# Two-layer hybrid backbone with expert-choice MoE: read-back of the residual streams tied to the last gather, final norm on one engine, output sums in one piece

## The chip, the cores and the metric

The kernel runs on one core of a Trainium2 chip. The metric is the device time of one execution, in microseconds (us). TensorE (PE), VectorE (DVE), ScalarE (ACT), GpSimd (POOL) and SyncE (SP) run their own queues in order and wait for each other through semaphores. Plain transfers here are issued by SP (queue q1 of the profile), the gathers, scatters and the read-back by POOL (queue q0); both use the same 16 DMA engines.

## The reference, cut to what matters

Two layers over 512 latent tokens and 256 context tokens of width 1024. A layer adds an attention and convolution branch to the streams, and then a mixture of experts: each of 16 experts takes the tokens for which its router score is highest (64 latent ones; in the first layer 32 context ones too), runs a SwiGLU on them, and its weighted rows are added to the tokens that they came from. The output is a last RMS norm.

```python
def ec_ffn(h, router_w, w_gate, w_up, w_down):
    aff = jax.nn.softmax((h @ router_w).astype(jnp.float32), axis=-1)
    top_aff, idx = lax.top_k(jnp.swapaxes(aff, 1, 2), cap)
    xg = jax.vmap(lambda hb, ib: hb[ib])(h, idx)                    # gather
    hid = jax.nn.silu(einsum(xg, w_gate)) * einsum(xg, w_up)
    y = einsum(hid, w_down) * top_aff[..., None]
    return zeros.at[idx].add(y)                                      # sum into the tokens
...
for li in range(2):
    xl = xl + g1 * (mix(xl, xc) @ w_o)
    xl = xl + g2 * ec_ffn(rmsnorm(xl, norm2_g) * (1 + sc2) + sh2, ...)   # xc alike, in layer 0 only
return rmsnorm(xl, final_norm_g)
```

## The kernel before, in words

All weights are float32 and are read once, in 1 MB pieces through a ring of slots; one expert has four pieces of gate and up (`load_gu`) and two of down (`load_d`). The order of TensorE's instructions is the order of the program; the other queues, SP's and POOL's among them, are ordered by a planner that runs through the program with estimated times and takes of the instructions that it thinks ready the one that stands first.

The expert part of a layer is one loop (e = 0 to 16, at the end of `layer`). Iteration e has on TensorE: `gate_up(e, 0)` (gate and up products of expert e for the latent rows); `hid_t(e-1)` (transposes of the hidden values of the expert before); a first `fill`; `columns(e+1)` (transposes of the gathered rows of the next expert into `xgT`); in layer 0 `gate_up(e, 1)` (context rows); a second `fill`; `down(e-1)` in `finish`. The rows of an expert are gathered by `gather` from a table in DRAM into `xg`, a single buffer: the gather for e+2 may start when `columns(e+1)` has read the one before. In layer 1 a gather and a `columns` serve two experts, so they stand in every second iteration only, `columns` in the odd ones.

There are two ways in which an expert's rows reach the streams. In layer 0 the experts 0 to 11 add theirs into copies of the streams in DRAM (`accs`), by a scatter that accumulates (lines 1072 and 1073). After that the six stream tiles `xl` (four) and `xc` (two), 512 KB each, are read back from `accs` by POOL's queue (line 1194). Experts 12 to 15 of layer 0, and all of layer 1, are summed on TensorE instead: `combine` makes pieces, each of two matmuls (tile `cb`, two buffers) with a one-hot matrix, and an addition into half a tile of the stream by VectorE (line 1118). Pieces wait in the list `todo`, and `fill(n)` issues n of them: eight pieces for a pair of experts, after each second expert.

In layer 0 the read-back stands in iteration 13, behind `gather(15)` in the program; the additions that need it begin in iteration 15. The planner put four of the six transfers ahead of that gather in POOL's queue.

After the last expert of layer 1, `final` does for each of four tiles: two pieces, the sum of squares on ScalarE, the factor `rs` (line 147, a power on POOL), the multiplication by `rs` and by the gain `fg` (it lies in the tile `xg`), and the store. Tiles 1 and 3 do the multiplication in one instruction of VectorE, tiles 0 and 2 in one of ScalarE and one of POOL.

Of the kernel before, what the change touches and what calls it, by code (L numbers as in the profile page):

```python
# [13 lines left out]
AF = mybir.ActivationFunctionType  # L14
OP = mybir.AluOpType
# [11 lines left out]
NE = 16  # L27
# [17 lines left out]
def hybrid_kernel(ctx: ExitStack, tc: tile.TileContext, a, out):  # L45
    nc = tc.nc
    V, S, G, PE, Q = nc.vector, nc.scalar, nc.gpsimd, nc.tensor, nc.sync
# [57 lines left out]
    def bcast(src, off, parts, n):  # L105

        return bass.AP(tensor=src.tensor, offset=src.offset + off, ap=[[0, parts], [1, n]])
# [34 lines left out]
    def rstd_of(ssq, n, inv):  # L142

        t = small.tile([128, 16], F32, name="rs_t")
        r = small.tile([128, 16], F32, name="rs_r")
        V.tensor_scalar(t[:, :n], ssq, inv, EPS, op0=OP.mult, op1=OP.add)
        G.tensor_tensor(r[:, :n], t[:, :n], mhalf[:, :n], op=OP.pow)  # L147
        return r
# [91 lines left out]
    def layer(li, ada):  # L240
        upd = li == 0
# [517 lines left out]
        @early(-30)  # L759
        def load_gu(e, q=Q):  # L760
            wgu = wgus[e] = []
            for w in ("exp_w_gate", "exp_w_up"):
                ws = []
                for k in range(0, KD, 4):
                    t = slot([128, 4, FF])
                    q.dma_start(t, a[w][li, e, k // 4])
                    ws += [t[:, i] for i in range(4)]
                wgu.append(ws)

        def load_d(e, q=Q):  # L770
            wd = wds[e] = []
            for k in range(0, 4, 2):
                t = slot([128, 2, D])
                q.dma_start(t, a["exp_w_down"][li, e, k // 2])
                wd += [t[:, 0], t[:, 1]]
# [5 lines left out]
        for r in range(len(streams)):  # L781
            t = rt.tile([128, D], F32, name=f"g1_{r}")
# [6 lines left out]
        for r, grp in enumerate(streams):  # L789
            t = rt.tile([48, len(grp) * 64], F32, name=f"affT{r}")  # L790
# [208 lines left out]
        xgs, xgTs = {}, {}  # L999

        def gather(e):
            if not upd and e % 2:
                return
            xg = xgs[e] = ex.tile([ng, D], F32, name="xg", bufs=1)
            c = e if upd else e // 2
            G.indirect_dma_start(out=xg, out_offset=None, in_=tabx[li],
                                 in_offset=bass.IndirectOffsetOnAxis(ap=gidx[:ng, c:c + 1], axis=0))

        def columns(e):

            if not upd and e % 2:
                xgTs[e] = xgTs[e - 1]
                return
            xg = xgs[e]
            xgT = xgTs[e] = ex.tile([128, KD, ng], F32, name="xgT")
            for k0 in range(0, KD, 4):
                ps = ps_tp()
                for k in range(4):
                    PE.transpose(ps[:, k * ng:(k + 1) * ng], xg[:, (k0 + k) * 128:(k0 + k + 1) * 128], ident[:ng, :ng])  # L1019
                for k in range(4):  # L1020
                    s, b = m.a2[:, k0 + k], m.b2[:, k0 + k]
                    n = CAPL if upd else ng
                    S.activation(xgT[:, k0 + k, :n], ps[:, k * ng:k * ng + n], AF.Identity, bias=b[:, 0:1], scale=s[:, 0:1])  # L1023
                    if upd:
                        V.tensor_scalar(xgT[:, k0 + k, n:], ps[:, k * ng + n:(k + 1) * ng], s[:, 1:2], b[:, 1:2],
                                        op0=OP.mult, op1=OP.add)
# [3 lines left out]
        def gate_up(e, r):  # L1030

            xgT, wgu = xgTs[e], wgus[e]
            ps = ps_mm()
            if r == 0:
                n = FF
                c0 = 0 if upd else (e % 2) * CAPL
                for k in range(KD):
                    for s in range(2):
                        mm(ps[64 * s:64 * s + 64, :], xgT[:, k, c0:c0 + CAPL], wgu[s][k], k == 0, k == KD - 1)
            else:  # L1040
                n = FF // 2
                for k in range(KD):
                    for q in range(4):
                        mm(ps[32 * q:32 * q + 32, :n], xgT[:, k, CAPL:],
                           wgu[q // 2][k][:, (q % 2) * n:(q % 2 + 1) * n], k == 0, k == KD - 1)
            gh = hids[e, r] = ex.tile([128, FF], F32, name="gh")
            S.activation(gh[64:128, :n], ps[0:64, :n], AF.Silu)  # L1047
            V.tensor_tensor(gh[0:64, :n], ps[64:128, :n], gh[64:128, :n], op=OP.mult)  # L1048

        def hid_t(e, r):  # L1050
            n = FF if r == 0 else FF // 2
            hid = hids[e, r]
            ps = ps_tp()
            for c in range(n // 128):
                PE.transpose(ps[:, c * 64:c * 64 + 64], hid[0:64, c * 128:(c + 1) * 128], ident[:64, :64])  # L1055
            hT = hTs[e, r] = ex.tile([128, n // 2], F32, name=f"hTe{r}")
            S.copy(hT, ps[:, :n // 2])  # L1057
# [66 lines left out]
        rs = range(len(streams))  # L1124
# [16 lines left out]
        def final(steps, p):  # L1141

            fg = p.tile([ng, D], F32, name="xg", bufs=1)
            Q.dma_start(fg, bcast(a["final_norm_g"], 0, 128, D))
            sq2 = p.tile([128, 4, 2], F32, name="sq2f", bufs=1)
            def block(tb):
                x = X["xl"][tb]
                for hf in range(2):
                    steps[2 * tb + hf]()
                    j = p.tile([128, 512], F32, name="gh")  # L1150
                    S.activation(j, x[:, hf * 512:(hf + 1) * 512], AF.Square, accum_out=sq2[:, tb, hf:hf + 1])
                sq = small.tile([128, 1], F32, name="ssq")
                V.tensor_tensor(sq, sq2[:, tb, 0:1], sq2[:, tb, 1:2], op=OP.add)
                rs = rstd_of(sq, 1, 1.0 / D)
                if tb % 2:
                    V.scalar_tensor_tensor(x, x, rs[:, 0:1], fg, op0=OP.mult, op1=OP.mult)  # L1156
                else:
                    S.activation(x, x, AF.Identity, scale=rs[:, 0:1])
                    G.tensor_tensor(x, x, fg, op=OP.mult)
                Q.dma_start(out[tb * 128:(tb + 1) * 128, :], x)  # L1160

            for tb in range(4):
                block(tb)

        def fill(n):
            for f in todo[:n]:
                f()
            del todo[:n]
# [5 lines left out]
        for e in range(NE + 1):  # L1174
            if e + 1 < NE and e + 1 not in wgus:
                load_gu(e + 1, G if upd and e == 1 else Q)
            if e < NE:
                if e not in wds:
                    load_d(e, Q if upd or e > 1 else G)
                gate_up(e, 0)  # L1180
            if e:
                for r in rs:
                    hid_t(e - 1, r)
                fill(3 if upd else 2)
            if e < NE:
                if e + 1 < NE:
                    columns(e + 1)
                if e + 2 < NE:
                    gather(e + 2)
                if upd and e == NE - 3:  # L1190

                    for x, acc in ((X["xl"], accs[0]), (X["xc"], accs[1])):
                        for i, t in enumerate(x):
                            G.dma_start(t, acc[i * 128:(i + 1) * 128, :])
                if upd:
                    gate_up(e, 1)
            if e:
                fill(3 if upd else 2)
                finish(e - 1)
        if upd:  # L1200
            fill(len(todo))
# [10 lines left out]
    with tc.manual_schedule(engines={mybir.EngineType.PE}):  # L1212
        for li in range(DEPTH):
            layer(li, ada)
# [93 lines left out]
```

## Time and profile before

Three runs took 1455.22, 1456.85 and 1459.57 us; the median is 1456.85 us. The profiled execution took 1453.06 us, of which its span from the first to the last instruction is 1451.3 us.

| engine or queue | busy us | share of the span |
|---|---|---|
| TensorE matmul | 1280.1 | 88% |
| TensorE weight load | 800.0 | 55% |
| VectorE | 687.3 | 47% |
| ScalarE | 517.6 | 36% |
| GpSimd | 242.2 | 17% |
| queue q1 (SP), of 16 DMA engines | | 50.7% |
| queue q0 (POOL), of 16 DMA engines | | 7.3% |

321.14 MB are moved, 221 GB/s over the span. The expert loop of layer 0 runs from about 523 to 848 us, that of layer 1 from about 1203 us to the end. A busy share is an average over stages with different limits; within a stage one looks for the wait that ended last.

### The profile page before, as it was taken

Reading aid. Unit: us, or ns where it says so; the run is one execution under the profiler, and the core shown is the slowest. Engines: PE = TensorE matmul, PEld = TensorE weight load, DVE = VectorE, ACT = ScalarE, POOL = GpSimd, SP = SyncE. Lnnn points to the kernel's source line nnn. Section 1 sums busy time; section 2 is a strip of 40 time slices with the busy share of each in tenths; the row PEclk is TensorE's granted clock in tenths of the full one; section 3 lists DMA queues with packets and bytes.
Section 4 is the critical chain, followed back from the end, with each engine's and each line's share of the span. In section 5 each row is a group of like instructions: output and inputs, shape, how many; then the busy total and the mean of one; then the engine's idle time right before and its main releaser. Section 6 shows DMA issues by size and latency. Waiting matters only on the chain. (4 is left out here: it accounts for less than half of the span.)

```text
span 1451.3 us, 21505 instructions
## 1 busy us (share of the span) xinstructions
PE 1280.1 (88%) x8542; PEld 800.0 (55%) x8542; DVE 687.3 (47%) x1516; ACT 517.6 (36%) x1095; POOL 242.2 (17%) x266
## 2 busy tenths in 40 slices
PE   3989989999999869999996969998999958999994
PEld 0768866666678624444443438876777843343331
DVE  1545356566743632222222474847776351333435
ACT  2523145455533322222222143436666322232222
POOL 1111001212210222222221020102232011111203
PEclk9989999999999979999998969999999978999998
DMA  8523315444732489999999310110012857999991
GB/s 355 187 99 116 149 63 215 175 182 182 291 145 82 190 314 361 367 373 370 373 371 399 133 56 32 71 62 1 1 41 70 341 222 308 419 418 420 419 416 62
DMA packets 56195, 321.14 MB, mean 221 GB/s; under 512 B 8720, under 2 KB 10384, under 8 KB 22560
## 3 DMA queue, kind: packets, MB, share of 16 engines
q1 hardware_dynamic: 45664, 286.75, 50.7%
q0 software_dynamic: 10432, 33.04, 7.3%
q8 instruction: 67, 1.10, 0.3%
q14 instruction: 32, 0.26, 0.1%
HBM read 304.52 MB, written 15.24 MB: 220 GB/s over the span
## 5 line engine op out<-in xcount | busy, mean ns | idle before, releaser
L59 PE MATMUL mm<-slot,xgT 128*64 128x512 f32 (+1 forms) x2048 | 290.6, 493 | 0.8 <-DMA slot<-in_exp_w_up_dram 0.7
L59 PE MATMUL mm<-hT,w 128*128 128x512 f32 (+1 forms) x1176 | 230.8, 356 | 3.0 <-POOL w L140 2.0
L59 PEld LDWEIGHTS mm<-hT,w 128*128 128x128 f32 x1176 | 192.6, 192 | 37.5 <-POOL w L140 2.4
L59 PEld LDWEIGHTS mm<-slot,xgT 128*64 128x64 f32 (+1 forms) x2048 | 104.8, 125 | 170.5 <-issue 143.8
L59 PE MATMUL mm<-slot,hTe 128*32 128x256 f32 (+1 forms) x1024 | 146.8, 490 | 0.8 <-ACT hTe L1057 0.8
L1048 DVE TENSOR_TENSOR gh<-mm,gh 64x512 f32<-64x512 f32 (+1 forms) x48 | 29.0, 604 | 218.4 <-ACT gh L1047 218.4
L1047 ACT ACTIVATE gh<-mm 64x512 f32<-64x512 f32 (+1 forms) x48 | 24.9, 518 | 278.1 <-PE tp L1055 171.8
L59 PE MATMUL mm<-wo,mixb 128*128 128x512 f32 x360 | 98.2, 409 | 2.3 <-DVE mixb L140 1.4
L59 PEld LDWEIGHTS mm<-slot,hTe 128*32 128x32 f32 (+1 forms) x1024 | 48.9, 123 | 88.7 <-issue 71.3
L694 ACT COPY pt<-tp 128x512 f32<-128x512 f32 (+1 forms) x120 | 64.9, 542 | 81.3 <-PE tp L691 80.2
L691 PE MATMUL tp<-ident,p 128*128 128x128 f32 x552 | 87.1, 283 | 5.5 <-ACT pt L694 2.3
L1023 ACT ACTIVATE xgT<-tp,modT,a 128x64 f32<-128x64 f32 (+1 forms) x192 | 70.1, 425 | 58.7 <-PE tp L1019 54.3
L681 POOL TENSOR_SCALAR p<-p,sm 128x768 f32<-128x768 f32 (+1 forms) x30 | 58.5, 1951 | 124.3 <-DVE sm L680 116.0
L691 PEld LDWEIGHTS tp<-ident,p 128*128 128x128 f32 x552 | 61.1, 142 | 27.1 <-issue 18.0
L59 PEld LDWEIGHTS mm<-wo,mixb 128*128 128x128 f32 x360 | 65.1, 191 | 16.2 <-DVE mixb L140 2.2
L59 PE MATMUL ada<-slot,sT 128*32 128x512 f32 x384 | 53.7, 678 | 22.9 <-DMA slot<-in_ada_w_dram 22.9
L59 PE MATMUL sc<-kt,qh 96*128 96x512 f32 (+1 forms) x324 | 69.7, 348 | 0.0
L139 ACT CAST w<-slot 128x1024 fp32r<-128x1024 f32 x30 | 31.4, 1046 | 100.1 <-PE mm L59 73.8
L59 PE MATMUL sc<-kst,qst 128*128 128x256 f32 (+1 forms) x288 | 48.2, 298 | 20.5 <-DVE mx L678 12.7
L670 DVE TENSOR_REDUCE mx<-sc 128x1 f32<-128x768 f32 (+1 forms) x60 | 51.0, 851 | 26.9 <-PE sc L59 25.9
L59 PE MATMUL cb<-yp,pl 128*128 128x512 f32 x160 | 53.1, 449 | 11.5 <-DVE xl L1118 9.2
L1101 POOL TENSOR_SCALAR pl<-tok,st 128x512 fp32r<-128x512 f32 (+1 forms) x21 | 32.9, 1575 | 171.9 <-PE cb L59 171.8
(246 smaller groups left out, 1772.9 us busy)
## 6 DMA issues: line engine op xcount, KB each, us to landing
slot<-in_exp_w_gate_dram SPq DMA_DIRECT2D x62, 1024.0 KB
slot<-in_exp_w_up_dram SPq DMA_DIRECT2D x62, 1024.0 KB
slot<-in_exp_w_down_dram SPq DMA_DIRECT2D x62, 1024.0 KB
slot<-in_ada_w_dram SPq DMA_DIRECT2D x48, 1024.0 KB
slot<-in_win_dram SPq DMA_DIRECT2D x14, 1024.0 KB
slot<-in_wo_dram SPq DMA_DIRECT2D x8, 1024.0 KB
tabx<-xn POOLq DMA_DIRECT2D x10, 512.0 KB
xt<-in_x_dram SPq DMA_DIRECT2D x4, 512.0 KB
```

The source lines that it names most:

```text
L59: PE.matmul(o, l, r, start=start, stop=stop, skip_group_check=True)
L139: (hi or V.tensor_copy)(out[0], x)
L670: V.tensor_reduce(mx, sc[:, :n], axis=AX.X, op=OP.max, negate=True)
L681: (G if s and self.kind == "mla" else V).tensor_scalar(p[:, :n], p[:, :n], sm, None, op0=OP.mult)
L691: PE.transpose(ps[:, b * 128:(b + 1) * 128], p[:, (b0 + b) * 128:(b0 + b + 1) * 128], ident)
L694: S.copy(o, ps[:, :n * 128])
L1023: S.activation(xgT[:, k0 + k, :n], ps[:, k * ng:k * ng + n], AF.Identity, bias=b[:, 0:1], scale=s[:, 0:1])
L1047: S.activation(gh[64:128, :n], ps[0:64, :n], AF.Silu)
L1048: V.tensor_tensor(gh[0:64, :n], ps[64:128, :n], gh[64:128, :n], op=OP.mult)
L1101: G.tensor_scalar(pl, tok[:, :nt], slots[r][:, g:g + 1], None, op0=OP.is_equal)
```

## The change

Three edits. `final` uses VectorE's one instruction for all four tiles. In the expert loop the first `fill` goes, and the second issues as many pieces as both did. The read-back of layer 0 moves from iteration 13 to 14, and ahead of each of its transfers VectorE copies one column of the transposed rows of expert 15 into the tile that is to be filled: the transfer overwrites that column, but has to wait for the copy, and the copy for `columns(15)`, which needs the gathered rows.

```diff
@@ final @@
-                if tb % 2:
-                    V.scalar_tensor_tensor(x, x, rs[:, 0:1], fg, op0=OP.mult, op1=OP.mult)
-                else:
-                    S.activation(x, x, AF.Identity, scale=rs[:, 0:1])
-                    G.tensor_tensor(x, x, fg, op=OP.mult)
+                V.scalar_tensor_tensor(x, x, rs[:, 0:1], fg, op0=OP.mult, op1=OP.mult)
                 Q.dma_start(out[tb * 128:(tb + 1) * 128, :], x)
@@ the loop over e @@
             if e:
                 for r in rs:
                     hid_t(e - 1, r)
-                fill(3 if upd else 2)
             if e < NE:
                 if e + 1 < NE:
                     columns(e + 1)
                 if e + 2 < NE:
                     gather(e + 2)
-                if upd and e == NE - 3:
+                if upd and e == NE - 2:
                     for x, acc in ((X["xl"], accs[0]), (X["xc"], accs[1])):
                         for i, t in enumerate(x):
+                            V.tensor_copy(t[:, 0:1], xgTs[NE - 1][:, 0, 0:1])
                             G.dma_start(t, acc[i * 128:(i + 1) * 128, :])
                 if upd:
                     gate_up(e, 1)
             if e:
-                fill(3 if upd else 2)
+                fill(6 if upd else 4)
                 finish(e - 1)
```

## Rows read from the trace of the kernel before

**Rows 1.** Waits, 700 to 850 us: engine line, releaser: total us, times, longest us.
```profile
PE tp L1019 <- DMA xg<-tabx,gidx: 10.9, 1, 10.9
PEld mm L59 <- DMA slot<-in_exp_w_up_dram: 1.9, 2, 1.0
```

**Rows 2.** Timeline of PE, layer 0: start, us, line, operation [idle before, releaser].
```profile
754.76 7.09 PE L59 MATMUL mm<-slot,xgT 128*64 128x512 f32 x32
...
762.29 0.55 PE L1019 MATMUL tp<-ident,xg 96*128 96x96 f32 x4
...
763.85 3.66 PE L59 MATMUL mm<-slot,xgT 128*32 128x256 f32 x64
...
772.89 8.48 PE L59 MATMUL mm<-slot,xgT 128*64 128x512 f32 x32
...
792.75 1.54 PE L1019 MATMUL tp<-ident,xg 96*128 96x96 f32 x8 [10.87 <-DMA xg<-tabx,gidx]
794.22 5.04 PE L59 MATMUL mm<-slot,xgT 128*32 128x256 f32 x64
...
814.30 0.73 PE L59 MATMUL cb<-yp,pl 128*128 128x512 f32 x2 [0.94 <-DVE xl L1118]
...
820.36 0.73 PE L59 MATMUL cb<-yp,pl 128*128 128x512 f32 x2 [0.59 <-DVE xl L1118]
```

**Rows 3.** Timeline of POOL, the same stretch.
```profile
746.06 0.95 POOL L1006 DMA_INDIRECT xg<-tabx,gidx  x1 [6.50 <-PE tp L1019]
...
763.94 2.24 POOL L1194 DMA_DIRECT2D xl<-acc  x4 [6.22 <-DMA acc<-ya,pi]
...
768.02 0.97 POOL L1006 DMA_INDIRECT xg<-tabx,gidx  x1 [0.30 <-issue]
```

**Rows 4.** DMA queues, 746 to 763, then 769 to 784: packets, MB, share.
```profile
q0 software_dynamic: 349, 0.74, 18.5%
...
q1 hardware_dynamic: 574, 4.18, 67.0%
q0 software_dynamic: 569, 2.07, 34.1%
```

**Rows 5.** Stretch: us, busy PE, PEld, DVE, ACT, POOL, PEclk, DMA, GB/s.
```profile
788.00:790.00 2.00, 0.00 (x0) 0.00 (x0) 0.00 (x0) 0.00 (x0) 0.00 (x0) 0.50 1.01 285
```

**Rows 6.** Timeline of DVE, the last sums of layer 0.
```profile
847.47 0.69 DVE L1118 TENSOR_TENSOR xc<-xc,cb 128x512 f32<-128x512 f32 x1 [0.46 <-PE cb L59]
```

**Rows 7.** Timeline of PE, layer 1.
```profile
1259.41 1.33 PE L59 MATMUL cb<-yp,pl 128*128 128x512 f32 x4 [0.67 <-DVE xl L1118]
...
1272.56 1.04 PE L1019 MATMUL tp<-ident,xg 128*128 128x128 f32 x8
...
1376.12 1.02 PE L59 MATMUL mm<-slot,xgT 128*64 128x512 f32 x2
1377.85 7.08 PE L59 MATMUL mm<-slot,xgT 128*64 128x512 f32 x30 [0.71 <-DMA slot<-in_exp_w_up_dram]
...
1421.82 1.33 PE L59 MATMUL cb<-yp,pl 128*128 128x512 f32 x4 [0.32 <-DVE xl L1118]
```

**Rows 8.** Waits of SP's queue, 1255 to 1400 us.
```profile
SPq L766 <- DMA slot<-in_exp_w_down_dram: 24.8, 12, 2.9
```

**Rows 9.** Timeline of all engines, the last 17 us.
```profile
1435.53 2.34 POOL L1159 TENSOR_TENSOR xl<-xl,xg 128x1024 f32<-128x1024 f32 x1
1435.60 3.35 DVE L1156 SCALAR_TENSOR_TENSOR xl<-xl,rs_r,xg 128x1024 f32<-128x1024 f32 x1
...
1437.90 6.81 SPq L1160 DMA_DIRECT2D out_dram<-xl  x4
1438.88 0.15 DVE L1153 TENSOR_TENSOR ssq<-sq2f 128x1 f32<-128x1 f32 x1
...
1440.40 1.28 DVE L1156 SCALAR_TENSOR_TENSOR xl<-xl,rs_r,xg 128x1024 f32<-128x1024 f32 x1 [0.93 <-POOL rs_r L147]
1441.10 2.77 POOL L1159 TENSOR_TENSOR xl<-xl,xg 128x1024 f32<-128x1024 f32 x1 [0.74 <-ACT xl L1158]
```

## The prediction

> **What bounds the kernel now.** I read the page first (TensorE is busy for 88% of the span), then the waits of the engines around the changed lines, then timelines there. The part that the change touches has three stages with different limits.
>
> Layer 0's experts run at TensorE's pace: one iteration takes 18.13 us (gate_up's start at 754.76 to the next at 772.89 [rows 2]), and the `columns` at 762.29 starts with no idle time ahead of it, as do those of the iterations before. There is one exception, the longest wait of the stage: 10.9 us, for gathered rows [rows 1]. It stands ahead of `columns(15)` at 792.75 [rows 2]. The cause is in POOL's queue [rows 3]: the gather for expert 14 was issued at 746.06, two microseconds after the columns before it began; the one for expert 15 could have gone at about 764.2, but four read-back transfers and a fifth were issued from 763.94 on, and the gather followed at 768.02, behind 2.6 MB on the same queue. From 769 to 784 us that queue got 2.07 MB in 15 us, 138 GB/s, while the weights on q1 got 4.18 MB, 279 GB/s [rows 4]. Five tiles of 0.524 MB and a gather of 0.39 MB at 138 GB/s are 22 us; from 768 that is 790, and TensorE went on at 792.75. So the read-back is what the gather waits for.
>
> Layer 1's experts are close to two limits at once: TensorE works without gaps, but SP's queue waits again and again for earlier transfers to land [rows 8], and at iteration 13 TensorE meets that limit for the first time, at 1377.85 [rows 7]. After it only arithmetic is left, and the tail is a chain of VectorE, POOL, ScalarE and the stores [rows 9].
>
> **The change part by part**, against the profiled execution (1453.06 us, span 1451.3 us; that lies 3.8 us under the median of the runs, so I take the difference from the median).
>
> *The read-back behind the gather.* The gather goes out at 764.2 and is needed 16.2 us later, the time that the gather for expert 14 had with q0 carrying 0.74 MB in the 17 us before [rows 3, 4]; with the read-back held back q0 carries less. So the idle 10.87 us go; the columns then take 1.56 us as at 762.29 to 763.85, not 1.47: 10.8 us. What ran behind the gap was slow too: the clock had fallen to 0.50 of full, 1.2 GHz, after TensorE had stood still for some microseconds [rows 5], and gate_up of the context rows took 5.04 us where it takes 3.66 [rows 2]: 1.4 us more. Ahead of the gap the product at 772.89 took 8.48 us instead of 7.09, with two waits for pieces of the up weights [rows 1, 2], in the stretch where q1 got only 279 GB/s. With q0 nearly empty q1 has over 100 GB/s more from 764 on; the 4.2 MB that q1 carried up to 777.7 are then in by about 775, and the second piece is needed at about 776. I take all 1.4 us (bounds 0 and 1.4).
>
> What is late next? The weights of expert 15 (4.2 MB behind those of 14) are in by about 787: 2.6 MB of them go at 410 GB/s before 781.5, the rest beside the read-back at 279. They are needed at 791. The read-back can start when `columns(15)` has filled its first column, about 781.5. At 138 GB/s a tile takes 3.8 us, so the first lands at about 785.5, the third at 793, the last at 804. The first addition needs tile 0 at about 803, the third tile is needed at 806, and the last one at 833 (847.47 [rows 6], shifted). Cover of over 12 us. The six copies on VectorE are near the smallest row, 0.15 us [rows 9], 0.9 us in all, at a time when VectorE has only the eviction of `xgT`; I take zero, with 0.9 as the bound. Behind the six transfers POOL has only the one-hot matrices of experts 14 and 15, whose buffers come free with those additions anyway. SP's queue keeps its order.
>
> *One `fill` of six in iteration 15.* Two runs of three pieces paid a wait each, 0.94 and 0.59 us [rows 2]; a run of six pays the first wait and then goes at VectorE's pace, some 0.75 us a piece. That makes about 4.7 us where there were 5.3: 0.6 us gained (bounds 0 and 1.5, none or both waits).
>
> *Four pieces in one run in layer 1.* In even iterations nothing stood between the two fills, so nothing changes there. In the odd ones the columns (1.04 us, with no wait behind them [rows 7]) gave VectorE time to free the buffers of `cb`. Now the columns come first and a wait stands between the second and the third piece: 0.67 us as in the even iterations, or 0.32 us as at 1421.82, where VectorE had no other product to do first [rows 7]. The ends overlap less as well; I take 0.55 us, bounds 0.32 and 0.85. Six odd iterations (3 to 13) have both columns and pieces: 3.3 us. Five come before TensorE meets the weights at 1376.12, where 32 products take 8.81 us, from 1376.12 to 1384.93 [rows 7] against 7.04 elsewhere. If the weights keep their own pace, those 1.77 us are absorbed. Net loss 1.5 us (bounds 0.3 and 3.3).
>
> *The last norm on VectorE.* Its instruction takes 1.28 us alone and took 3.35 beside POOL's [rows 9]. Before, tile 2 went through ScalarE and then 2.77 us on POOL, which ended at 1443.87, and tile 3, ready since 1441.68, stood behind it in SP's queue; the last store was issued by 1444.71 [rows 9]. Now from 1434.1 VectorE has two additions of 0.69 us, some 0.6 us of small steps and four products of 1.28: 7.1 us, so 1441.2 if it never idles, and the store is issued by 1441.6, 3.1 us sooner. Only one tile instead of two is then left to move, which is up to 1.25 us more (0.524 MB at 418 GB/s). I take 3.7 us (bounds 2 and 4.2; 2 if the small steps wait behind products).
> The row shows two engines at work on the same tiles, one of them held up: 3.35 us is 1.28 plus nearly the rest of POOL's 2.34. The Trainium skill (SBUF — State Buffer, section Who interferes with whom) says why this may not be over: a VectorE instruction with two SBUF inputs and a GpSimd one that reads SBUF exclude each other for their whole length. By that, each power for `rs` on POOL could wait out a product on VectorE, which makes the gain of the tail about 2.5 instead of 3.7 us, and the sum 15.2.
>
> Sum: 10.8 + 1.4 + 1.4 + 0.6 = 14.2 in layer 0, less 1.5 in layer 1, plus 3.7 in the tail: 16.4 us less. Between the two expert stages nothing has a time of its own: layer 1 begins with the streams that layer 0's last sums give, and the weights that it needs first are issued tens of microseconds before. So the profiled execution would be at 1436.7, and the median at 1456.85 - 16.4 = 1440.5 us.
>
> **The rivals.**
> *POOL's powers and VectorE's products shut each other out in the tail.* For it: the 3.35 us [rows 9]. Against: the powers are some 0.55 us long and three of them can run before the last sums end. Time 1441.7.
> *The gap shrinks but doesn't close.* The rows of expert 15 come some microseconds late all the same, or the weights of expert 15 take their place, as DMA is busy without a break. For it: the 1.9 us of waits for weights [rows 1], and weights in by 787 where 791 is wanted. Against: the gather before had the same 16.2 us. Half of the gap with its slow clock is 6 us: 1446.5.
> *The change doesn't do what it says.* The gather is late through the weights, not through the read-back. Then the 13.6 us of gap, clock and weights stay and 0.6 + 3.7 - 1.5 = 2.8 us remain: 1454. Against it speaks the arithmetic with 138 GB/s.
> *The other side: the read-back itself becomes the wait.* All its 3.15 MB start 17.6 us later than before. If q0 got no more than in the regular iterations (0.74 MB in 17 us, 44 GB/s [rows 4], which was all that it was asked for), they would take 72 us from 781.5, to 854, where the last tile is wanted at 833. That is 20.7 us lost against 16.4 gained: 1461. It decides below about 46 GB/s; against it stand the 138 GB/s that the same transfers got.
>
> **How the numbers follow.** My forecast has 0.63, the exclusion in the tail 0.12, the half-closed gap 0.14, no effect on the gap 0.06, the late read-back 0.05. The bounds of the terms give 11.5 to 19 us for the forecast, 1438 to 1445.5; the runs spread by some 2 us around their median, and the half-closed gap reaches to 1449. The range is 1434 to 1449. A difference under 0.3%, 4.4 us, can't be told from none: faster means below 1452.5, which the first three cases are (0.89); same is the fourth (0.06); slower the last (0.05).
>
> **What would show it.** In the profile after, the gather of expert 15 is issued near 764 and `columns(15)` starts near 780.5 with no idle time; gate_up behind it takes 3.66 us, the product ahead of it 7.1; the read-back is issued near 782 and no addition into `xl` or `xc` waits for DMA; the odd iterations of layer 1 have a wait of 0.3 to 0.7 us in the run of pieces, and the wait at iteration 13 is gone; in the tail no VectorE product takes over 2 us and the last store is issued 6 to 7 us after the last sum. I am wrong if TensorE waits for gathered rows, weights or stream tiles for more than 2 us between 764 and 848, or if layer 1's stage grows by over 3.3 us.

## The result, and the profile after

Twelve runs of each kernel on one chip: 1455.97 us before, 1441.31 us after (medians). The ratio is 0.9897, 95% interval 0.988 to 0.9914: faster by 15.0 us, 12.5 to 17.5 (the two medians differ by 14.7). The forecast was 16.4 us less, 1440.5.

The profiled execution after took 1440.98 us, its span is 1438.5 us. To see where the difference lies, the span is cut at four starts on TensorE: the `gate_up` of expert 13 in layer 0, the first transpose of layer 1 (line 333), the first `columns` of layer 1, and its last `gate_up`. This table has all kernels of this study, one trace of each (us, differences of starts in each timeline; the kernels behind the second row are told of under the experiments):

| kernel | to gate_up(13) | A: to layer 1's first transpose | B: to its first columns | C: to its last gate_up | D: to the end |
|---|---|---|---|---|---|
| before | 754.76 | 97.91 | 350.22 | 202.95 | 45.46 |
| after | 757.70 | 85.64 | 348.74 | 203.90 | 42.52 |
| tie alone | 760.02 | 85.74 | 348.62 | 204.15 | 45.87 |
| norm alone | 756.77 | 97.70 | 350.55 | 206.26 | 41.82 |
| one fill alone | 757.64 | 96.96 | 352.00 | 205.04 | 45.46 |
| after, layer 1 with two fills | 759.10 | 85.71 | 348.93 | 203.76 | 42.60 |
| moved without tie | 756.44 | 97.75 | 350.47 | 203.30 | 45.44 |
| read-back later still | 757.09 | 90.48 | 349.89 | 205.13 | 42.61 |
| no read-back | 756.09 | 86.65 | 352.39 | 205.07 | 44.60 |
| after, no scatters | 755.33 | 83.40 | 348.44 | 203.65 | 40.38 |

Stage A gives 12.3 us and stage D 2.9; C takes back 1.0. The first column and B hold no line that the change touches; over the ten traces they differ by 5.3 and 4.0 us and are spoken of at the end.

POOL's queue after, same columns as [rows 3]: the gather of expert 15 goes out at 767.14, and the read-back 21 us later.

```profile
767.14 0.95 POOL L1006 DMA_INDIRECT xg<-tabx,gidx  x1 [6.52 <-PE tp L1019]
788.17 2.21 POOL L1190 DMA_DIRECT2D xl<-acc  x4 [20.08 <-DVE xl L1189]
790.34 1.09 POOL L1190 DMA_DIRECT2D xc<-acc  x2
```

TensorE's timeline after, beside [rows 2] (`hid_t` behind the product of expert 14 starts at 785.31):

```profile
775.83 1.07 PE L59 MATMUL mm<-slot,xgT 128*64 128x512 f32 x2
778.30 7.08 PE L59 MATMUL mm<-slot,xgT 128*64 128x512 f32 x30 [1.40 <-DMA slot<-in_exp_w_up_dram]
...
785.83 0.55 PE L1019 MATMUL tp<-ident,xg 96*128 96x96 f32 x4
...
787.39 3.66 PE L59 MATMUL mm<-slot,xgT 128*32 128x256 f32 x64
...
807.56 1.20 PE L59 MATMUL cb<-yp,pl 128*128 128x512 f32 x4
809.36 1.33 PE L59 MATMUL cb<-yp,pl 128*128 128x512 f32 x4 [0.60 <-DVE xl L1118]
810.88 1.33 PE L59 MATMUL cb<-yp,pl 128*128 128x512 f32 x4 [0.18 <-DVE xl L1118]
```

`columns(15)` at 785.83 has no idle time ahead of it, where 10.87 us stood; the `gate_up` behind it takes 3.66 us, not 5.04. But the product ahead of it, which had lost 1.4 us to late weights in the trace of before, takes from 775.83 to 785.38, 9.55 us where 7.1 is regular: TensorE still loses 2.5 us there. Whether that is more than before can't be read from one pair of traces; the ten together follow below. The six pieces in one run show one wait of 0.60 and one of 0.18, and no addition waits for a stream tile. The waits after, 700 to 850 us, are in the form of [rows 1]: TensorE's row for gathered rows is gone, and a wait for up weights stays, on its weight loads (PEld) and its products (PE). POOL's wait is the tie at work: the transfers wait for the copies.

```profile
POOL xl L1190 <- DVE xl L1189: 20.1, 1, 20.1
...
PEld mm L59 <- DMA slot<-in_exp_w_up_dram: 2.3, 1, 2.3
...
PE mm L59 <- DMA slot<-in_exp_w_up_dram: 1.4, 1, 1.4
```

The queues after, from 798 to 803 us, while the read-back passes beside the weights [rows 4]: 0.81 MB in 5 us, 162 GB/s. The two queues have about as many packets each, 222 and 178; q0's are the smaller ones.

```profile
q1 hardware_dynamic: 178, 1.29, 62.1%
q0 software_dynamic: 222, 0.81, 40.3%
```

TensorE in layer 1 after [rows 7]: an odd iteration (1289.62), where the wait of 0.32 us now stands behind the columns, an even one, and iteration 13 (1367.57 on), which has no wait for weights.

```profile
1289.62 1.09 PE L1019 MATMUL tp<-ident,xg 128*128 128x128 f32 x8
...
1291.96 1.33 PE L59 MATMUL cb<-yp,pl 128*128 128x512 f32 x4 [0.32 <-DVE xl L1118]
...
1362.82 1.33 PE L59 MATMUL cb<-yp,pl 128*128 128x512 f32 x4 [0.70 <-DVE xl L1118]
...
1367.57 7.04 PE L59 MATMUL mm<-slot,xgT 128*64 128x512 f32 x32
```

The tail after, all engines [rows 9]:

```profile
1424.96 1.28 DVE L1155 SCALAR_TENSOR_TENSOR xl<-xl,rs_r,xg 128x1024 f32<-128x1024 f32 x1
...
1426.27 6.49 SPq L1156 DMA_DIRECT2D out_dram<-xl  x4
...
1427.02 0.67 DVE L1118 TENSOR_TENSOR xl<-xl,cb 128x512 f32<-128x512 f32 x1
...
1427.12 1.07 POOL L147 TENSOR_TENSOR rs_r<-rs_t,mhalf 128x1 f32<-128x1 f32 x2 [2.40 <-DVE rs_t L146]
...
1427.71 2.48 DVE L1155 SCALAR_TENSOR_TENSOR xl<-xl,rs_r,xg 128x1024 f32<-128x1024 f32 x2
...
1430.10 0.15 DVE L1153 TENSOR_TENSOR ssq<-sq2f 128x1 f32<-128x1 f32 x1
...
1430.52 0.55 POOL L147 TENSOR_TENSOR rs_r<-rs_t,mhalf 128x1 f32<-128x1 f32 x1 [2.34 <-DVE rs_t L146]
1431.11 1.29 DVE L1155 SCALAR_TENSOR_TENSOR xl<-xl,rs_r,xg 128x1024 f32<-128x1024 f32 x1 [0.66 <-POOL rs_r L147]
```

All four products take 1.24 to 1.29 us. The last store is issued by 1432.76 and the span ends 5.7 us later, where it was 6.6 [rows 9]: one tile instead of two to move. VectorE isn't busy throughout, which the forecast had assumed: tile 0's product went ahead of the last additions, and the small steps of tile 3 waited behind two products, so that the last product waits 0.66 us for its power. The last store is issued 5.1 us after the last sum (1427.69), not 6 to 7 as forecast, because tile 0's product no longer stands behind it.

### The profile page after: what moved, and what is told of

It is laid out like the page before. It is cut to its first block, busy times and chain, and to the rows that moved or that the text cites. A ratio compares the mean times of both kernels' runs of the same rounds, so it can differ in the third digit from the quotient of the medians.

```text
span 1438.5 us, 21510 instructions
## 1 busy us (share of the span) xinstructions
PE 1280.0 (89%) x8542; PEld 799.4 (56%) x8542; DVE 688.0 (48%) x1524; ACT 515.8 (36%) x1093; POOL 237.2 (16%) x264
## 5 line engine op out<-in xcount | busy, mean ns | idle before, releaser
L59 PEld LDWEIGHTS sc<-kt,qh 96*128 96x128 f32 x324 | 52.6, 190 | 10.0 <-issue 3.4
```

The costliest lines, as they stand in the source:

```text
L59: PE.matmul(o, l, r, start=start, stop=stop, skip_group_check=True)
```

## The experiments

**The three edits, each alone.** Their ratios multiply to 0.990, the whole change's 0.9897: no interaction shows, within their intervals.

*The tie alone* (fills and norm as before):

```diff
-                if upd and e == NE - 3:
+                if upd and e == NE - 2:
                     for x, acc in ((X["xl"], accs[0]), (X["xc"], accs[1])):
                         for i, t in enumerate(x):
+                            V.tensor_copy(t[:, 0:1], xgTs[NE - 1][:, 0, 0:1])
                             G.dma_start(t, acc[i * 128:(i + 1) * 128, :])
```

> The tied read-back alone, fills and last norm as before. Theory A (the gather stood behind the read-back in POOL's queue): the 10.9 us gap ahead of columns(15) goes, the product behind it runs at full clock, and nothing waits for the stream tiles: 11 to 13 us less than before, ratio 0.991 to 0.9925. Theory B (weights or the late read-back take the gap's place): TensorE shows a new wait for weights or xl tiles between 764 and 848 us that adds up to more than 4 us, ratio above 0.995.

Measured: ratio 0.9924 (0.99 to 0.9949), 11 us. Stage A is 12.2 us shorter. The stages behind it, which this edit doesn't touch, differ from before by 0.4 to 1.6 us and sum to nothing (B 1.6 shorter, C 1.2 and D 0.4 longer). Theory A.

*The norm alone:*

```diff
-                if tb % 2:
-                    V.scalar_tensor_tensor(x, x, rs[:, 0:1], fg, op0=OP.mult, op1=OP.mult)
-                else:
-                    S.activation(x, x, AF.Identity, scale=rs[:, 0:1])
-                    G.tensor_tensor(x, x, fg, op=OP.mult)
+                V.scalar_tensor_tensor(x, x, rs[:, 0:1], fg, op0=OP.mult, op1=OP.mult)
```

> The last norm on VectorE alone. Theory A (the tail is the stores behind POOL's long product): from the start of the last gate_up product to the end of the span about 2.9 us less than before (45.5 us there), all earlier stages alike, ratio near 0.998. Theory B (POOL's powers and VectorE's products exclude each other): some product takes over 1.8 us, or a power over 1 us, and the tail gains under 2 us.

Measured: ratio 0.9977 (0.9963 to 0.999), 3.3 us. Stage D is 41.82 us, 3.6 less than before; no product in the tail takes over 1.3 us, no power over 0.6. Theory A; the exclusion between POOL's powers and VectorE's products doesn't show here either, as in the tail above.

*One fill alone:*

```diff
                     hid_t(e - 1, r)
-                fill(3 if upd else 2)
...
-                fill(3 if upd else 2)
+                fill(6 if upd else 4)
```

> The sums in one piece alone. Theory A: in layer 0 0.6 us less; in layer 1 each odd iteration with columns 0.45 us longer, six of them, and the weights wait at iteration 13 (1.8 us) absorbed: about 1 us more there, so ratio 1.000 within 0.001. Theory B (the weights follow TensorE's pace through the slots): the wait at iteration 13 stays and the layer loses 2.7 us, ratio near 1.0015.

Measured: ratio 0.9998 (0.9981 to 1.0016). Stage A is 0.95 us shorter. Stage C is 2.1 us longer: 0.9 in the iterations, as theory A says, and 1.2 in the first products of the layer, which this edit doesn't touch (16.06 us, 14.87 before; the granted clock was 0.65 there from 1210 to 1214, and 0.92 before from 1206 to 1210). In stage C iteration 13 starts at 1383.23 in this kernel and has no wait for weights:

```profile
1383.23 7.04 PE L59 MATMUL mm<-slot,xgT 128*64 128x512 f32 x32
```

against the kernel with the tie alone, whose layer 1 is the old one:

```profile
1367.67 1.02 PE L59 MATMUL mm<-slot,xgT 128*64 128x512 f32 x2
1370.54 7.08 PE L59 MATMUL mm<-slot,xgT 128*64 128x512 f32 x30 [1.85 <-DMA slot<-in_exp_w_up_dram]
```

There 32 products take 9.95 us instead of 7.04. The odd iterations come 0.45 us later each, and when iteration 13 is reached the weights are there: Theory A.

**The changed kernel with layer 1's two fills back:**

```diff
                     hid_t(e - 1, r)
+                if not upd:
+                    fill(2)
...
-                fill(6 if upd else 4)
+                fill(6 if upd else 2)
```

> The changed kernel with layer 1's two fills of two pieces put back (layer 0 keeps its one fill of six). Theory A: the odd iterations of layer 1 are 0.45 us shorter again, the wait for the up weights at iteration 13 is back with 1 to 2 us, and the stage from the first columns of layer 1 to the last gate_up is 1 us shorter than in the changed kernel: 1440 us, ratio 0.989. Theory B: no wait comes back: 2.7 us shorter, ratio 0.988.

Measured: ratio 0.9885 (0.9865 to 0.9906), against 0.9897 for the change: not told apart. The wait for weights is back (32 products in 9.69 us, 2.65 too long), and stage C is 203.76 us, 0.14 less than in the changed kernel, not 1: Theory A in kind, with a longer wait than it said. Over the ten traces, stage C is 203.0 to 206.3 us with two fills in layer 1 and 203.7 to 205.1 with one. With one fill the six odd iterations take 14.44 us instead of 13.98, 2.7 us in all; with two, iteration 13 loses 1.8 to 5.1 us at the weights (the table below), with one 0 to 0.9. What the one order costs is about what the other loses to weights.

**Is it the tie, or the place in the program?** The read-back moved to iteration 14, without the copies:

```diff
-                if upd and e == NE - 3:
+                if upd and e == NE - 2:
```

> The read-back stands in iteration 14 of the program instead of 13, without the copies that tie it; fills and norm as before. Theory A (the planner issues whatever it thinks ready, so only the data dependence moves the read-back): POOL issues read-back transfers ahead of the gather for expert 15 as before, the wait ahead of columns(15) is 9 to 12 us, the time that of before. Theory B (the place in the program is enough): the gather is issued first, the wait is gone and 12 us with it.

One run: 1455.18 us. POOL's queue has the order of before, four transfers of `xl` and a fifth, of `xc`, ahead of the gather (before, too, it was five, the fifth at 767.18, where the words on the kernel say four), though the gather now stands a whole iteration earlier in the program:

```profile
765.64 2.24 POOL L1194 DMA_DIRECT2D xl<-acc  x4 [6.51 <-DMA acc<-ya,pi]
768.79 0.53 POOL L1194 DMA_DIRECT2D xc<-acc  x1 [0.91 <-DMA acc<-ya,pi]
769.63 0.97 POOL L1006 DMA_INDIRECT xg<-tabx,gidx  x1 [0.30 <-PE mm L59]
```

TensorE waits 7.0 us for the rows, less than the 9 to 12 of theory A (10.9 us before, 9.2 with the norm alone, 9.3 with one fill alone), but it has lost 5.0 us at the weights just before:

```profile
774.58 1.07 PE L59 MATMUL mm<-slot,xgT 128*64 128x512 f32 x2
777.92 8.78 PE L59 MATMUL mm<-slot,xgT 128*64 128x512 f32 x30 [2.27 <-DMA slot<-in_exp_w_up_dram]
...
794.25 1.54 PE L1019 MATMUL tp<-ident,xg 96*128 96x96 f32 x8 [7.04 <-DMA xg<-tabx,gidx]
```

The two together are 12.1 us, against 12.3 before, and stage A is 97.75 us, as before. When the rows land is set in POOL's queue, and what TensorE loses ahead of them only shortens its wait for them. Theory A: the place in the program doesn't move the transfers, the data dependence does.

**Is the read-back the cause?** The kernel before, without its six read-back transfers (the sums of experts 0 to 11 of layer 0 don't reach the streams):

```diff
-                if upd and e == NE - 3:
-                    for x, acc in ((X["xl"], accs[0]), (X["xc"], accs[1])):
-                        for i, t in enumerate(x):
-                            G.dma_start(t, acc[i * 128:(i + 1) * 128, :])
```

> The kernel before without the read-back (the sums of experts 0 to 11 of layer 0 are left out of the streams). Theory A (the read-back is what the gather waits for): no wait ahead of columns(15). On the two waits for the up weights of expert 14, together 1.4 us before and 2.5 us with the change: Theory A1 (they come from the read-back's share of the DMA engines): none here. Theory A2 (the weights are already behind, since the loop asks for as much as the engines move): 1 to 3 us here as well. Theory B: the gather is late by itself: 5 us or more ahead of columns(15).

One run: 1446.88 us. The gap ahead of `columns(15)` is gone, stage A is 86.65 us. But of TensorE's waits from 700 to 850 us one for the up weights of expert 14 is there all the same:

```profile
PE mm L59 <- DMA slot<-in_exp_w_up_dram: 1.6, 1, 1.6
```

The 32 products take 9.80 us, 2.8 too long, without any read-back. So that wait doesn't need the read-back: Theory A2, not A1.

**Then what makes those weights late?** The changed kernel without the accumulating scatters of layer 0 (the rows are computed and not added):

```diff
-                G.indirect_dma_start(out=accs[r].rearrange("t (q c) -> (t q) c", q=np_),
-                                     out_offset=bass.IndirectOffsetOnAxis(ap=places_of[r][:, e:e + 1], axis=0),
-                                     in_=t, in_offset=None, compute_op=OP.add)
```

> The changed kernel without the accumulating scatters of experts 0 to 11 in layer 0 (their rows are computed but not added). Theory A2 on the weights wait of expert 14 (the scatters' small packets hold the weights back, 370 GB/s moved in the loop against 420 elsewhere): the wait at the start of gate_up(14) is gone and the loop of layer 0 up to there runs at 18.1 us an iteration; 1 to 2.5 us gained against the changed kernel. Theory C (the wait comes from the ring of slots, SP asking too late): it stays at 1 us or more.

One run: 1433.33 us. The products of expert 14 run without a wait:

```profile
773.46 7.09 PE L59 MATMUL mm<-slot,xgT 128*64 128x512 f32 x32
```

The queues of the changed kernel from 749 to 766 us, with scatters:

```profile
q1 hardware_dynamic: 761, 5.51, 83.5%
q0 software_dynamic: 353, 0.74, 18.5%
```

and of this one in the same stretch, without them:

```profile
q1 hardware_dynamic: 888, 6.50, 94.6%
q0 software_dynamic: 86, 0.29, 4.9%
```

The engines are busy throughout in both (the shares add up to 102 and 99.5%). With 0.45 MB less on q0, q1 moves 1.0 MB more: 382 GB/s instead of 324. A full iteration asks for six pieces of 1.05 MB in 18.13 us, 347 GB/s. Over a longer stretch, 540 to 640 us, q1 carries 32.79 MB with the scatters and 34.75 without, 328 and 348 GB/s. So with the scatters the weights fall behind by some 20 GB/s. In that stretch SP's queue waits only for TensorE to free a slot, in both kernels. From 640 to 760 us it also waits for earlier pieces to land, 25.1 us in all after the change, of which this is the longest row,

```profile
SPq L766 <- DMA slot<-in_exp_w_up_dram: 8.5, 5, 3.2
```

and without the scatters this is all:

```profile
SPq L766 <- DMA slot<-in_exp_w_down_dram: 0.3, 1, 0.3
```

That the stock in the ring is used up by expert 14 follows from these rows; it was not measured piece by piece. Stage A is 2.2 us shorter than after the change, about the 2.5 us of that wait. Theory A2; theory C, that SP asks too late, is refuted.

What the ten traces say of the weights together (us; what TensorE loses at the product of expert 14 in layer 0, from its start to the transposes behind it, over the regular 7.0; the wait for gathered rows right behind; and the loss at iteration 13 of layer 1; each figure rounded by itself):

| kernel | expert 14 | rows | both | layer 1, iteration 13 |
|---|---|---|---|---|
| before | 1.4 | 10.9 | 12.3 | 1.8 |
| norm alone | 2.9 | 9.2 | 12.0 | 5.1 |
| one fill alone | 3.2 | 9.3 | 12.5 | 0 |
| moved without tie | 5.0 | 7.0 | 12.1 | 2.2 |
| no read-back | 2.7 | 0 | 2.7 | 2.9 |
| after | 2.5 | 0 | 2.5 | 0 |
| tie alone | 1.9 | 0 | 1.9 | 2.9 |
| after, layer 1 with two fills | 1.8 | 0 | 1.8 | 2.7 |
| read-back later still | 2.4 | 0 | 2.4 | 0.9 |
| after, no scatters | 0 | 0 | 0 | 0.2 |

In the four kernels with the read-back ahead of the gather the loss at expert 14 varies from 1.4 to 5.0 us, and the wait for rows makes up the difference. The profiled execution of before, from which the prediction took its 1.4, has the smallest loss of the four.

**How much cover does the read-back have?** The changed kernel with the read-back tied to expert 15's hidden values:

```diff
-                if upd and e == NE - 2:
+                if upd and e == NE - 1:
...
-                            V.tensor_copy(t[:, 0:1], xgTs[NE - 1][:, 0, 0:1])
+                            V.tensor_copy(t[0:64, 0:1], hids[NE - 1, 0][0:64, 0:1])
```

> The changed kernel with the read-back one iteration later still: it stands in iteration 15, and the copies read expert 15's hidden values, so its transfers start some 4 us ahead of the first sum that needs them (about 18 us later than in the changed kernel). Theory A (the six transfers pass at 120 to 160 GB/s beside the weights, 3.3 to 4.4 us each, at up to 400 GB/s without them; the changed kernel has 12 us of cover): TensorE waits for the first and second tiles, 3 to 8 us in all, ratio 0.992 to 0.995. Theory B (the landing of the read-back is never near the path): nothing lost, ratio 0.990.

Measured: ratio 0.9952 (0.9917 to 0.9987). The transfers start at 805.14 on POOL; VectorE's first addition is released by DMA:

```profile
811.64 1.28 DVE L1118 TENSOR_TENSOR xl<-xl,cb 128x512 f32<-128x512 f32 x2 [3.72 <-DMA xl<-acc]
```

and TensorE stands 4.29 us in the run of pieces:

```profile
812.38 3.82 PE L59 MATMUL cb<-yp,pl 128*128 128x512 f32 x8 [4.29 <-DVE xl L1118]
```

Stage A is 4.8 us longer than after the change. The first tile lands 6.5 us after its issue, which came 2.8 us before the addition was due (807.92) and not some 4 as meant, and the others stay ahead of their additions. Theory A in kind, with one wait, not two. In the changed kernel the issue, at 788.17, is 20 us ahead of the first addition (808.62). If the first tile takes 6.5 us there too, that is some 14 us of cover; this is an estimate, since no wait marks the landing in that trace. What q0 moves there, 0.15 MB from 788 to 793 us and 0.75 from 793 to 798, makes it some 13 if the tiles of 0.52 MB pass one after the other.

## Why the prediction was right, point by point

*What the gather waited for: right and shown.* Taking the read-back away closes the gap; moving it in the program alone doesn't; tying it does. The gap (10.8 us) and the slow clock behind it (1.4 us: 5.04 to 3.66 us, granted clock 0.50 in the gap [rows 5], 1.00 from 784 to 796 after) came as forecast.

*The weights of expert 14: this step failed.* "With q0 nearly empty q1 has over 100 GB/s more from 764 on" gave 1.4 us; in truth TensorE lost 2.5 us there after the change, and 1.8 to 2.5 in all four kernels with the tie and the scatters. That is over the 2 us of waits between 764 and 848 that the prediction itself gave as a sign of being wrong. Two things were wrong. First, q1 had no such room: in the changed kernel it carried 1.79 MB from 772 to 778 us, 298 GB/s, hardly more than beside the read-back [rows 4], and both queues together 346 GB/s, not 418. The weights were behind before the read-back began: the loop asks for nearly all that the engines move while the accumulating scatters run, and the wait at expert 14 is there in all nine kernels with scatters, 1.4 to 5.0 us, with or without a read-back. Second, the 1.4 us were no term of their own. Before, the loss at the weights and the wait for rows were 12.0 to 12.5 us together, whatever the share of each; without the wait for rows, the loss at the weights stays, and the change gives the difference.

*The read-back's own cover: right*, over 12 us said, some 14 estimated from the trial, which started 2.8 us ahead and cost 4.3 us. The rival in which the read-back becomes the wait is refuted: no addition waited for it, and it moved at 162 GB/s beside the weights from 798 to 803 us.

*The fill in layer 0: right* (0.6 said; the pieces took 5.3 and now 4.6 us). Another 0.45 us of stage A lie behind it, from the start of `down(14)` (821.02 before, 812.14 after) to layer 1's first transpose: 31.65 and 31.20 us. They can't be put down to the change, since the ten traces have 31.2 to 32.0 us there.

*Layer 1: right in mechanism.* An odd iteration is 0.45 us longer (0.55 said), and the wait at iteration 13 is gone in exchange. The net 1.5 us was 1.0 in this pair of traces, in which before has the smallest loss at the weights of all kernels with two fills (1.8 of 1.8 to 5.1 us). The two experiments don't tell the orders apart, so the edit has no price of its own here that these runs can measure.

*The tail: right*, 3.7 said; stage D gave 2.9 with the whole change and 3.6 with the norm alone. In both the last product waits 0.66 us for its power. The 0.7 us between the two go with the clock in the last pieces: the granted clock is 0.78 from 1419 to 1423 us in the changed kernel, and 1.00 in the stretch with the same pieces in before (1430 to 1434) and with the norm alone (1434 to 1438). The rule of the Trainium skill (SBUF — State Buffer, Who interferes with whom), on which one rival rests, fits the row of before, where the product beside POOL's took 3.35 us. Beside a power it didn't show: the one product that ran beside one after the change (1427.71 on, beside the second of two powers) kept its 1.28 us, so the rival built on it fell.

So the sum of 16.4 us missed by 1.4 us (1.7 by the medians), against an interval 5 us wide: the weights' term was 2.5 us too good and the others within 0.8 us. That the total came so near is in part luck, as the untouched stages alone differ by more from trace to trace. Two bounds of the prediction are added up wrongly, and the stated range doesn't rest on them: the lower one for layer 1 is 6 x 0.32 less 1.77, 0.15 us and not 0.3, and the lower one of the sum 10.8 + 1.4 - 3.3 + 2, 10.9 us and not 11.5.

## What to carry to other kernels

Before a wait for a small, urgent transfer is put down to bandwidth, look at what was issued ahead of it on the same queue: here 0.39 MB stood behind 2.6. Where a planner orders the queue, a place in the program may not decide the order; a data dependence did here, and a copy of one column is a cheap one (0.14 us each) if it can stand beside other work. A wait next to the fault need not share its cause: two waits 10 us apart here had two, which only leaving one transfer out could tell. And two waits in a row, of which the second ends with a landing that the first doesn't move, are one sum: what the first loses the second gives back, so here the first was worth nothing while the second stood behind it.

## What the runs showed of the hardware that was not expected

Runs of one program spread by some 1%, and TensorE's granted clock goes with it: of the twelve runs after, the fastest took 1435.12 us at a mean granted clock of 0.961 and the slowest 1449.79 us at 0.948. Stages that no edit touched differ with it. Stage B is 350.22 us before and 352.00 with one fill alone, though all queues have the same instruction order there. The clock changes at different places in the two. These are two stretches that begin 13.3 and 13.4 us after the first transpose of layer 1 (us, busy PE, PEld, DVE, ACT, POOL, granted clock, DMA share, GB/s), of before:

```profile
866.00:868.00 2.00, 2.00 (x11) 1.90 (x10) 0.84 (x2) 0.94 (x2) 0.00 (x0) 0.50 0.01 4
```

and with one fill alone:

```profile
868.00:870.00 2.00, 2.00 (x15) 1.59 (x13) 1.93 (x4) 1.43 (x3) 0.00 (x0) 1.00 0.01 4
```

After some idle time one execution is back at 2.4 GHz while the other is still at 1.2 GHz. The kernel whose stage is longer in the end is the one ahead here, and at 980.47 (the same matmul is at 980.82 before) it is 2.3 us ahead within the stage. Up to the transposes at 1000.59 (before at 998.91) it then loses 2.0 us, and the levels are the other way round, with one fill alone

```profile
992.00:996.00 4.00, 3.54 (x18) 2.41 (x17) 2.63 (x6) 2.84 (x7) 0.00 (x0) 0.50 0.01 2
```

and before

```profile
990.00:994.00 4.00, 2.95 (x32) 2.64 (x31) 3.50 (x7) 3.68 (x7) 0.29 (x2) 1.00 0.03 8
```

It loses another 1.3 us from 1089.55 to 1094.01, with 0.74 from 1088 to 1092, where before has 1.00 (1086 to 1090). What decides when the clock rises or falls was not tried. A comparison of two traces is therefore read stage by stage, and the total only over many runs.

Beside the weights the accumulating scatters cost more than their bytes: with the engines busy throughout, leaving out 0.45 MB of them in 17 us let 1.0 MB more of weights through.
